# Hymba block on one core: scores of head group B over 128 rows with zeroed partner rows, one softmax factor on ScalarE, adaLN tiles packed closer

## The chip, the core and the metric

One core of a Trainium2 chip runs one launch of the kernel. The metric is the device time in microseconds, taken as the median over runs. Five engines matter here: the tensor engine (PE, with PEld for its weight loads), VectorE (DVE), ScalarE (ACT), GpSimd (POOL) and SyncE (SP, which issues most DMAs). Each works through its own queue in order, and semaphores join them.

## The reference

One decoder layer over 512 tokens, model width 2048, all in 32-bit floats. Eight heads of group A use dilated windows; eight heads of group B use differential attention, which is where the change lies:

```python
def differential_attention(q, k, v, lam):
    # q, k: (B, S, 2, H, e): two maps, e = 64; v: (B, S, H, 128)
    ...
        s = jnp.einsum('bqmhe,bkmhe->bmhqk', qblk, k)        # one block of 128 queries
        s = jnp.where(causal, s, -jnp.inf)
        a = jax.nn.softmax(s, axis=-1)
        attn = a[:, 0] - lam * a[:, 1]
        return jnp.einsum('bhqk,bkhe->bqhe', attn, vf)
...
mod = silu(c) @ w_ada + b_ada                                # adaLN: six vectors of 2048
h = rmsnorm(x, g_pre_attn) * (1.0 + sc_a) + sh_a
proj = h @ w_in                                              # q, k, v of both groups
...                                                          # rope, both attentions, per-head rmsnorm
x = x + gt_a * rmsnorm(mix @ w_out, g_post_attn)
h = rmsnorm(x, g_pre_ffn) * (1.0 + sc_f) + sh_f
x = x + gt_f * rmsnorm((silu(h @ w_gate) * (h @ w_up)) @ w_down, g_post_ffn)
```

A score of group B thus contracts over 64 numbers, and every head has two score maps.

## The kernel before

**Large products.** Weights and activations are split into a rounded part and a rest (`w_hi` on ScalarE at L1709, `w_lo` on VectorE at L1718), and each product is three fast ones (L277 to L279 with the activations stationary, L282 to L284 with the weights stationary). Attention itself works in plain 32-bit floats.

**Steps.** After a first phase the program is a list of steps. A projection step (0 to 79) takes one 128x1024 weight tile and issues 24 fast products of 512 columns; an output-projection step (80 to 143) issues 12; then comes the feed-forward part. The main loop at the end of `body` writes each step in this order: things that start a step (`start_ev`, among them the copies of finished projections to SBUF and the DMAs that swap rows for the rotary part), attention on the tensor engine (`pe_ev`), the first half of the step's products, the split on ScalarE for the tile two steps ahead (`do_hi`), transposes and copies (`mid_ev`, `mid_act`), the second half, then VectorE's work (`post_ev`, `post_late`, `do_lo`), then the small adaLN tiles (`aux`), then `post_end`. Nothing reorders afterwards, so an engine's queue stands in this order.

**Attention units.** `place_unit` puts a unit into a step. For group B a unit is one block of 128 queries of one head: head h, block b stands in step 20 + 4h + b, so the 32 units fill steps 20 to 51. `unit_stages` gives its parts. `s0` (same step, ahead of the step's products): the two score products (L507; head h uses rows 64(h mod 2) to 64(h mod 2)+63 of its pair's tile for both maps), mask and maximum on VectorE (L512), exponential with its sum on ScalarE (L516). `s0b` (late in the step) is

```python
dve.reciprocal(stt[:, 6:8], stt[:, 4:6])                                  # L521
dve.tensor_scalar(stt[:, 0:1], stt[:, 7:8], nlam, None, op0=OP.mult)      # L522: the factor of map 1
dve.tensor_scalar(p1(), p1(), stt[:, 0:1], None, op0=OP.mult)             # L523
dve.scalar_tensor_tensor(p0(), p0(), stt[:, 6:7], p1(), ...)              # L524
```

One step later come the transposes (L529) and their copy (L534), two steps later the value products (L545, first thing on the tensor engine). When a head's last block is done, `head_post` normalises it: copy (L558), largest value, squares on ScalarE (L568), four small operations (L581 to L584), and a step later the scaling (L589, L590), its transposes later still (L595). For head h the copy, the squares and the four small operations fall into the step of block 1 of head h+1, and on VectorE they stand ahead of that block's factor.

**Rotary.** `evac_rope_at` makes three long VectorE operations (L426 to L428) per half pair of heads. A planner puts them into steps 17, 18, 22, 23, 25, 26, 30, 34, 46 and 50 within group B's stretch, ahead of that step's factor.

**adaLN tiles.** 96 tiles of 512 KB (and 32 more much later) are multiplied and summed on VectorE (L228). They share a ring of four `raw` buffers with the weights, in the order of their use. The same planner adds them to steps while its running estimate of VectorE's time stays within `M_ADA` of the tensor engine's (`M_ADAW` from step 80 on); its estimates per unit are in `place_unit`. Steps 0 to 10 also hold late shift tiles with VectorE work of their own, steps 4 to 14 a correction (L728).

**Tables.** `tabB` (made in `late_tab` at step 14) has four planes of 512 columns: cosine, sine, causal mask, and one unused.

Of the kernel before, what the change touches and what calls it, by code (L numbers as in the profile page):

```python
# [8 lines left out]
AF = mybir.ActivationFunctionType  # L9
OP = mybir.AluOpType  # L10
# [11 lines left out]
LATE_KC = [KORDER[s] for s in LATE_S]  # L22
KORDER2 = [kc for kc in KORDER if kc not in LATE_KC] + LATE_KC
M_ROPE = 1.0
M_ADA = -0.05
M_ADAW = 0.8
M_AV = -1.0
M_DMA = 0.7
# [6 lines left out]
def body(tc, t):  # L35
    nc = tc.nc
    pe, act, dve, pool, sync = nc.tensor, nc.scalar, nc.vector, nc.gpsimd, nc.sync
# [3 lines left out]
    with ctx:  # L41
# [8 lines left out]
        def U(tag, shape, dt=F, name=None):  # L50
            return up.tile(shape, dt, tag=tag, name=name or tag)

        def PS(b, shape=(128, 512)):
            return pp.tile(list(shape), F, tag=f"b{b}", name=f"b{b}")
# [275 lines left out]
        QK = {}  # L330
# [62 lines left out]
        tabB = {}  # L393
# [78 lines left out]
        def pt_store(head, i):  # L472
            u, c = PT_AT[head, i]
            if u not in pts:
                pts[u] = U(PT_UNIT[u], [128, 2048], name=f"pts{u}")
            return pts[u][:, c:c + (384, 384, 512)[i]]

        def unit_stages(n, kind, head, qbs):
            W = sum(128 * (qb + 1) for qb in qbs)
            offs = [0, 128][:len(qbs)]  # L480
            d = {}
            p0 = lambda: misc["p"][:, n % 2, :W]
            p1 = lambda: misc["p"][:, 2 + n % 2, :W]
            last = kind == "A" and head >= 4

            def s0():
                stt = sp.tile([128, 8], F, name="stt", tag="stt", bufs=4)
                d["st"] = stt
                lst = []
                for j, qb in enumerate(qbs):  # L490
                    N = 128 * (qb + 1)
                    qs = slice(128 * qb, 128 * qb + 128)
                    ms_ = slice(128 * (3 - qb), 512)
                    r = slice(offs[j], offs[j] + N)
                    if kind == "A":
                        if j == 0:
                            sc = PS(4 + n % 2)
                        qk = QK[f"A{head // 2}"]
                        i = 2 * (head % 2)
                        pe.matmul(sc[:, r], qk[:, i, qs], qk[:, i + 1, :N], start=True, stop=True)  # L500
                        lst.append((sc[:, r], p0()[:, r], lc[:, ms_], SCALE_A, HEADST[kind, head]["den"][:, qb:qb + 1]))
                    else:
                        qk = QK[f"B{head // 2}"]
                        k = slice(64 * (head % 2), 64 * (head % 2) + 64)
                        for m in range(2):
                            sc = PS(4 + m)
                            pe.matmul(sc[:, :N], qk[k, 2 * m, qs], qk[k, 2 * m + 1, :N], start=True, stop=True)  # L507
                            lst.append((sc[:, :N], p0() if m == 0 else p1(), tabB["t"][:, 2, ms_], SCALE_B,
                                        stt[:, 4 + m:5 + m]))
                for m, (sc, p, mask, scale, den) in enumerate(lst):  # L510
                    mx = stt[:, m:m + 1]
                    dve.tensor_tensor_reduce(p, sc, mask, op0=OP.add, op1=OP.max, scale=1.0,  # L512
                                             scalar=-3e38, accum_out=mx)
                    nm = stt[:, 2 + m:3 + m]
                    dve.tensor_scalar(nm, mx, -scale, None, op0=OP.mult)
                    act.activation(p, p, AF.Exp, bias=nm, scale=scale, accum_out=den)  # L516

            def s0b():
                if kind == "B":
                    stt = d["st"]  # L520
                    dve.reciprocal(stt[:, 6:8], stt[:, 4:6])  # L521
                    dve.tensor_scalar(stt[:, 0:1], stt[:, 7:8], nlam, None, op0=OP.mult)  # L522
                    dve.tensor_scalar(p1(), p1(), stt[:, 0:1], None, op0=OP.mult)  # L523
                    dve.scalar_tensor_tensor(p0(), p0(), stt[:, 6:7], p1(), op0=OP.mult, op1=OP.add)  # L524

            def s1():
                tr = PS(6, (128, 4, 128))
                for j in range(W // 128):
                    pe.transpose(tr[:, j, :], misc["p"][:, n % 2, 128 * j:128 * j + 128], ident)  # L529
                d["tr"] = tr  # L530

            def s1b():
                d["pt"] = pt_store(head, max(qbs) - 1) if last else misc["pt"][:, n % 2, :W]
                act.activation(d["pt"], d["tr"][:, :W // 128, :], AF.Copy)  # L534

            def s2():
                h = HEADST[kind, head]
                if qbs[0] == 0:
                    h["pv"] = PS(head if last else 7, (128, 4, 128))
                v = V[f"V{kind}{head // 4}"]  # L540
                e = slice(128 * (head % 4), 128 * (head % 4) + 128)
                o = 0
                for qb in qbs:
                    for j in range(qb + 1):
                        pe.matmul(h["pv"][:, qb, :], d["pt"][:, o:o + 128], v[:, j, e], start=j == 0, stop=j == qb)  # L545
                        o += 128
            return s0, s0b, s1, s1b, s2

        HEADST = {}
# [52 lines left out]
        pe_cost = defaultdict(float)  # L602
        dve_cost = defaultdict(float)

        def place_unit(n, kind, head, qbs, hn, s):
            s0, s0b, s1, s1b, s2 = unit_stages(n, kind, head, qbs)
            m = 1 if kind == "A" else 2
            for qb in qbs:
                N = 128 * (qb + 1)
                pe_cost[s] += m * max(0.218, 0.00168 * N)  # L610
                dve_cost[s] += m * (0.4 + N / 960) + (1.0 + 1.6 * N / 960 if kind == "B" else 0)
                pe_cost[s + 1] += 0.107 * (qb + 1)
            if 0 in qbs:
                def mk(kind=kind, head=head):
                    h = HST[kind, head]
                    hs = sp.tile([128, 5, 4], F, name="hst", tag="hst", bufs=4)
                    for i, k in enumerate(("den", "ss", "f", "rd", "nb")):
                        h[k] = hs[:, i, :]
                pe_ev[s].append((0, mk))
            pe_ev[s].append((2, s0))  # L620
            post_late[s].append(s0b)
            mid_ev[s + 1].append(s1)
            mid_act[s + 1].append(s1b)
            if kind == "A" and head >= 4:
                late_pv[head].append(s2)
                assert s + 1 < W0
                return
            for qb in qbs:
                pe_cost[s + 2] += 0.218 * (qb + 1)
            pe_ev[s + 2].append((0, s2))  # L630
            if 3 in qbs:
                a, b, c, c2, d = head_post(kind, head, hn)
                start2_ev[s + 2].append(a)
                mid_act[s + 2].append(b)
                post_late[s + 2].append(c)
                post_ev[s + 3].append(c2)
                pe_ev[s + 4].append((1, d))
                dve_cost[s + 2] += 1.0 if kind == "A" else 1.6
                dve_cost[s + 3] += 0.8
                pe_cost[s + 4] += 0.43  # L640
# [18 lines left out]
        post_end = defaultdict(list)  # L659
# [102 lines left out]
        for part in range(2):  # L762
            start_ev[14 + part].append(lambda part=part: late_tab(part))
# [6 lines left out]
        def late_tab(part):  # L770
            if part == 0:
                tabB["t"] = U("R3", [128, 4, 512], name="tabB")
                sync.dma_start(tabB["t"][:, 2, :], t["cb"])
            for p in range(0, 128, 32):
                o = 64 * ((p // 32) % 2) if part else 0
                sync.dma_start(tabB["t"][p:p + 32, part, :], (sin_a if part else cos_a)[o:o + 64:2, :])
# [92 lines left out]
        for jj, kp in enumerate(KP_ORDER):  # L869
            for k in range(2):  # L870
                kc = 2 * kp + k
                s = wsteps[0, 0, jj, 0]
# [177 lines left out]
        for h in range(4, 8):  # L1050
            s = W0 + 1 + (h - 4)
# [4 lines left out]
        for i in range(W0 + 60):  # L1056
            mm_t = 5.13 if i < W0 else 2.57
            if todo:
                hn, k, h, qbs = todo[0]
# [20 lines left out]
            t_dma = max(t_dma, t_pe) + 1.45 * (1 + len(aux[i]))  # L1080
            while ada_todo and i < W0 + 46 and i >= 1 and t_dve + 1.14 <= t_end + (M_ADA if i < W0 else M_ADAW) and \
                    t_dma + 1.45 <= t_end + M_DMA and len(aux[i]) < NAUX:
# [554 lines left out]
        for c in range(2):  # L1637
            p = dpos
# [137 lines left out]
        for i in range(NSTEP):  # L1776
# [10 lines left out]
            s = steps[i]  # L1787
# [146 lines left out]
```

## Time and profile before

| What | Value |
|---|---|
| median of 3 runs | 2191.88 us (2189.95 to 2193.71) |
| profiled execution, its span | 2191.79 us, 2190.0 us |
| tensor engine busy | 2150.6 us |
| VectorE, ScalarE, GpSimd busy | 1672.8, 1058.8, 103.7 us |
| steps 20 to 51 (group B's units) | about 229 to 484 us |
| steps 80 to 143 (output projection) | about 677 to 870 us |

Times on the timeline count from the span's start. In a timeline row stand the start, the duration, engine and line, what is written and read, shapes, how many instructions were merged (the duration is then that of all), and in brackets the idle time before it with what ended it. A 32-bit product appears as two instructions. Matmuls overlap by more than a third of a recorded duration, so distances between starts say how long the engine was taken. Rows of groups give count, busy time and mean nanoseconds.

### The profile page before, as it was taken

The page shows a single profiled execution, that of the slowest core. Times are in us where ns is not written, and L with a number is a line of the kernel's source. Part 1 is how long each engine was busy: PE and PEld are TensorE (multiplying, and loading weights), DVE is VectorE, ACT ScalarE, POOL GpSimd, SP SyncE. Part 2 cuts the span into 40 slices and gives each one's busy share as a digit, 9 for nine tenths or more (in the row PEclk, how much of TensorE's full clock was granted, in tenths as well). Part 3 has the DMA queues.
Part 4 walks back from the last instruction along what each step waited for, and adds up shares of the span by engine and source line. Part 5 has one row for each costly group of instructions (what it writes and reads, how often), then busy time and mean ns, then how long its engine had stood idle before and what let it go on. Part 6 is the DMA issues. An engine that isn't in the chain of part 4 may idle for free.

```text
span 2190.0 us, 26905 instructions
## 1 busy us (share of the span) xinstructions
PE 2150.6 (98%) x9748; PEld 1756.7 (80%) x9748; DVE 1672.8 (76%) x2337; ACT 1058.8 (48%) x1541; POOL 103.7 (5%) x112
## 2 busy tenths in 40 slices
PE   7999999999999999999999999999999999999997
PEld 6888777778888888787888888888888888888886
DVE  6987777776767775796777677777777787798888
ACT  5444344444435565654555554555554544443443
POOL 0000000001001000000001011000100000000000
PEclk8999999999999999999999999999999999999999
DMA  9797634555678877888779769778877889999997
GB/s 374 297 347 228 167 113 155 167 155 175 215 232 272 291 248 255 265 284 231 221 219 281 227 203 278 221 209 253 250 220 213 278 332 396 337 386 362 345 338 268
DMA packets 160452, 564.39 MB, mean 258 GB/s; under 512 B 17440, under 2 KB 17728, under 8 KB 153920
## 3 DMA queue, kind: packets, MB, share of 16 engines
q1 hardware_dynamic: 142608, 502.09, 63.8%
q0 software_dynamic: 10944, 39.85, 10.3%
q10 hardware_dynamic: 6768, 20.73, 3.2%
q8 instruction: 77, 1.26, 0.2%
q14 instruction: 55, 0.45, 0.1%
HBM read 499.67 MB, written 54.02 MB: 253 GB/s over the span
## 4 chain that ended last, share of the span: by engine, by line
PE 87%; DMA 5%; DVE 5%; ACT 1%; issue 1%; ACTq 0%; POOL 0%; SPq 0%; DVEq 0%; POOLq 0%
PE b L283 22%; PE b L282 22%; PE b L284 22%; PE b L277 5%; PE b L279 5%; PE b L278 5%; PE b L507 2%; DMA w_raw<-in_wout 1%; DMA a<-acts 1%; DVE w_lo L1718 1%; PE b L545 1%; PE b L1276 1%; PE b L500 1%; PE b L529 1%; ACT w_hi L1709 1%
## 5 line engine op out<-in xcount | busy, mean ns | idle before, releaser
L1718 DVE TENSOR_TENSOR w_lo<-raw,w_hi 128x1024 fp32r<-128x1024 f32 x235 | 285.6, 1221 | 150.6 <-ACT w_hi L1709 150.3
L1709 ACT ACTIVATE w_hi<-raw 128x1024 fp32r<-128x1024 f32 x235 | 248.4, 1061 | 287.6 <-PE b L284 227.3
L282 PE MATMUL b<-w_hi,h 128*128 128x512 f32 x864 | 342.8, 397 | 0.4 <-ACT xT L212 0.4
L283 PE MATMUL b<-w_lo,h 128*128 128x512 f32 x864 | 337.0, 390 | 1.6 <-DVE w_lo L1718 1.5
L284 PE MATMUL b<-w_hi,h 128*128 128x512 f32 x864 | 336.9, 390 | 0.0
L1718 DVE TENSOR_TENSOR w_lo<-w_raw,w_hi 128x1024 fp32r<-128x1024 f32 x176 | 214.0, 1220 | 61.7 <-ACT w_hi L1709 61.6
L1709 ACT ACTIVATE w_hi<-w_raw 128x1024 fp32r<-128x1024 f32 x176 | 185.5, 1056 | 154.3 <-PE b L284 68.8
L282 PE MATMUL b<-w_hi,e 128*128 128x512 f32 x640 | 250.3, 391 | 3.9 <-ACT w_hi L1709 3.9
L283 PE MATMUL b<-w_lo,e 128*128 128x512 f32 x640 | 250.5, 391 | 0.6 <-DVE w_lo L1718 0.6
L284 PE MATMUL b<-w_hi,e 128*128 128x512 f32 x640 | 250.0, 391 | 0.0
L282 PE MATMUL b<-w_hi,a 128*128 128x512 f32 x616 | 240.1, 390 | 1.2 <-DMA a<-acts 1.2
L283 PE MATMUL b<-w_lo,a 128*128 128x512 f32 x616 | 240.0, 390 | 1.1 <-DVE w_lo L1718 1.1
L284 PE MATMUL b<-w_hi,a 128*128 128x512 f32 x616 | 239.8, 389 | 0.0
L277 PE MATMUL b<-h,w_hi 128*128 128x512 f32 x512 | 213.2, 416 | 0.0
L1709 ACT ACTIVATE w_hi<-w_lent 128x1024 fp32r<-128x1024 f32 x121 | 128.3, 1061 | 161.8 <-PE b L284 119.7
L278 PE MATMUL b<-h,w_hi 128*128 128x512 f32 x512 | 200.7, 392 | 2.9 <-DVE h L273 2.9
L279 PE MATMUL b<-h,w_lo 128*128 128x512 f32 x512 | 201.1, 393 | 0.0
L282 PEld LDWEIGHTS b<-w_hi,h 128*128 128x128 f32 x864 | 162.3, 188 | 37.1 <-issue 3.7
L283 PEld LDWEIGHTS b<-w_lo,h 128*128 128x128 f32 x864 | 162.4, 188 | 36.3 <-DVE w_lo L1718 3.4
L1718 DVE TENSOR_TENSOR w_lo<-w_lent,w_hi 128x1024 fp32r<-128x1024 f32 x121 | 147.5, 1220 | 55.3 <-ACT w_hi L1709 55.2
L284 PEld LDWEIGHTS b<-w_hi,h 128*128 128x128 f32 x864 | 162.2, 188 | 34.1
L282 PEld LDWEIGHTS b<-w_hi,e 128*128 128x128 f32 x640 | 120.8, 189 | 29.5 <-ACT w_hi L1709 4.4
(356 smaller groups left out, 3456.7 us busy)
## 6 DMA issues: line engine op xcount, KB each, us to landing
a<-acts SPq DMA_DIRECT2D x154, 512.0 KB, 5.2
raw<-in_wgu SPq DMA_DIRECT2D x131, 512.0 KB, 6.2
w_raw<-in_win SPq DMA_DIRECT2D x107, 512.0 KB, 5.0
w_raw<-in_adar SPq DMA_DIRECT2D x96, 512.0 KB, 4.6
w_lent<-in_wgu SPq DMA_DIRECT2D x69, 512.0 KB, 7.0
w_raw<-in_wout SPq DMA_DIRECT2D x64, 512.0 KB, 4.5
acts<-stage SPq DMA_DIRECT2D x49, 512.0 KB, 4.4
raw<-in_wds SPq DMA_DIRECT2D x47, 512.0 KB, 5.9
```

The costliest lines, as they stand in the source:

```text
L277: pe.matmul(ps, whi, ahi, start=start, stop=False, **kw)
L278: pe.matmul(ps, whi, alo, start=False, stop=False, **kw)
L279: pe.matmul(ps, wlo, ahi, start=False, stop=stop, **kw)
L282: pe.matmul(ps, ahi, whi, start=start, stop=False, **kw)
L283: pe.matmul(ps, ahi, wlo, start=False, stop=False, **kw)
L284: pe.matmul(ps, alo, whi, start=False, stop=stop, **kw)
L500: pe.matmul(sc[:, r], qk[:, i, qs], qk[:, i + 1, :N], start=True, stop=True)
L507: pe.matmul(sc[:, :N], qk[k, 2 * m, qs], qk[k, 2 * m + 1, :N], start=True, stop=True)
L529: pe.transpose(tr[:, j, :], misc["p"][:, n % 2, 128 * j:128 * j + 128], ident)
L545: pe.matmul(h["pv"][:, qb, :], d["pt"][:, o:o + 128], v[:, j, e], start=j == 0, stop=j == qb)
L1709: act.activation(hi, raw, AF.Copy)
L1718: dve.tensor_tensor(lo, raw, hi.bitcast(F), op=OP.subtract)
```

## The change

The fourth plane of `tabB` holds zeros in rows 64 to 127 of its first 256 columns (for even heads) and in rows 0 to 63 of the others (odd heads). At the end of the step before a unit, ScalarE copies the unit's query rows (64 rows, two maps of 128 columns) into the other half, and the score products contract over all 128 rows: the other head's keys meet zeros. The factor of map 1 is multiplied in by ScalarE. The planner's costs for group B's units are lowered and `M_ADA` goes from -0.05 to 0.5.

```diff
-M_ADA = -0.05
+M_ADA = 0.5
...
+        def qz_of(head):
+            return tabB["t"][:, 3, 256 * (head % 2):256 * (head % 2) + 256].rearrange("p (m q) -> p m q", m=2)
+
+        def qz_copy(head, qb):
+            k = slice(64 * (head % 2), 64 * (head % 2) + 64)
+            q = QK[f"B{head // 2}"].rearrange("p (m i) t -> p m i t", m=2)[k, :, 0, 128 * qb:128 * qb + 128]
+            act.activation(qz_of(head)[k], q, AF.Copy)
...
-                        k = slice(64 * (head % 2), 64 * (head % 2) + 64)
                         for m in range(2):
                             sc = PS(4 + m)
-                            pe.matmul(sc[:, :N], qk[k, 2 * m, qs], qk[k, 2 * m + 1, :N], start=True, stop=True)
+                            pe.matmul(sc[:, :N], qz_of(head)[:, m, :], qk[:, 2 * m + 1, :N], start=True, stop=True)
...
-                    dve.tensor_scalar(p1(), p1(), stt[:, 0:1], None, op0=OP.mult)
+                    act.activation(p1(), p1(), AF.Copy, scale=stt[:, 0:1])
...
-                pe_cost[s] += m * max(0.218, 0.00168 * N)
-                dve_cost[s] += m * (0.4 + N / 960) + (1.0 + 1.6 * N / 960 if kind == "B" else 0)
+                pe_cost[s] += m * max(0.222, (0.00168 if kind == "A" else 0.0009) * N)
+                dve_cost[s] += m * (0.4 + N / 960) + (0.8 + 0.8 * N / 960 if kind == "B" else 0)
...
+            if kind == "B":
+                post_end[s - 1].append(lambda: qz_copy(head, qbs[0]))
...
+                pool.memset(tabB["t"][64:128, 3, 0:256], 0.0)
+                pool.memset(tabB["t"][0:64, 3, 256:512], 0.0)
```

Twelve lines are added, so line numbers of the changed kernel are up to 12 higher. The units and the rotary steps stay in their steps. Of the 96 early adaLN tiles six move: steps 87, 88, 90, 91, 93 and 94 lose one each, steps 1, 2, 3, 13, 20 and 21 get one more.

ScalarE in step 25 (head 1, block 1), before: two exponentials, copy of head 0's result, split of a weight, squares, copy of transposes; then the next step's exponentials.

```order
L516 ACTIVATE misc_p,stt<-misc_p,stt 128x256 x2
L558 ACTIVATE misc_pt<-b_1900 128x512
L1709 ACTIVATE w_hi<-w_raw 128x1024
L568 ACTIVATE junk,hst<-misc_pt,hst 128x128 x4
L534 ACTIVATE misc_pt<-b_2105 128x128
L516 ACTIVATE misc_p,stt<-misc_p,stt 128x384 x2
```

The same place now:

```order
L524 ACTIVATE misc_p,stt<-misc_p,stt 128x256 x2
L566 ACTIVATE misc_pt<-b_1923 128x512
L1721 ACTIVATE w_hi<-w_raw 128x1024
L576 ACTIVATE junk,hst<-misc_pt,hst 128x128 x4
L542 ACTIVATE misc_pt<-b_2131 128x128
L531 ACTIVATE misc_p<-misc_p,stt 128x256
L485 ACTIVATE tabB<-B_950 64x256
L524 ACTIVATE misc_p,stt<-misc_p,stt 128x384 x2
```

The product by the factor (L531) and, behind it, the copy of the next unit's query rows (L485) stand between this step's work and the next step's exponentials.

VectorE in step 20 (head 0, block 0), from the reciprocal to the next unit's maximum, before:

```order
L521 RECIPROCAL stt<-stt 128x2
L522 TENSOR_SCALAR stt<-stt,lam_79 128x1
L523 TENSOR_SCALAR misc_p<-misc_p,stt 128x128
L524 SCALAR_TENSOR_TENSOR misc_p<-misc_p,stt 128x128
L1718 TENSOR_TENSOR w_lo<-w_raw,w_hi 128x1024
L228 SCALAR_TENSOR_TENSOR w_raw,red<-w_raw,silu_b 128x1024
L512 ISA misc_p,stt<-b_1850,tabB 128x256
```

and now:

```order
L529 RECIPROCAL stt<-stt 128x2
L530 TENSOR_SCALAR stt<-stt,lam_79 128x1
L532 SCALAR_TENSOR_TENSOR misc_p<-misc_p,stt 128x128
L1730 TENSOR_TENSOR w_lo<-w_raw,w_hi 128x1024
L228 SCALAR_TENSOR_TENSOR w_raw,red<-w_raw,silu_b 128x1024
L228 SCALAR_TENSOR_TENSOR w_raw,red<-w_raw,p_82 128x1024
L520 ISA misc_p,stt<-b_1869,tabB 128x256
```

L523 has left VectorE, so the operation behind it (now L532) waits for ScalarE, and a second adaLN tile (L228) has come in.

VectorE in the output projection, from the scaling of the last group A head on (steps 86 to 90), before:

```order
L590 TENSOR_TENSOR misc_p<-misc_p,hst 128x512
L228 SCALAR_TENSOR_TENSOR w_raw,red<-w_raw,silu_b 128x1024
L1718 TENSOR_TENSOR w_lo<-w_raw,w_hi 128x1024
L228 SCALAR_TENSOR_TENSOR w_raw,red<-w_raw,p_82 128x1024
L1718 TENSOR_TENSOR w_lo<-w_raw,w_hi 128x1024
L843 TENSOR_TENSOR mixlo_5203<-mixT_5538,mixhi_5202 128x256 x2
L228 SCALAR_TENSOR_TENSOR w_raw,red<-w_raw,silu_b 128x1024
L1718 TENSOR_TENSOR w_lo<-w_raw,w_hi 128x1024 x2
```

and now:

```order
L598 TENSOR_TENSOR misc_p<-misc_p,hst 128x512
L228 SCALAR_TENSOR_TENSOR w_raw,red<-w_raw,silu_b 128x1024
L1009 TENSOR_TENSOR red<-red 128x16
L1014 TENSOR_TENSOR gsh<-red,cst 128x16
L1730 TENSOR_TENSOR w_lo<-w_raw,w_hi 128x1024 x2
L855 TENSOR_TENSOR mixlo_5255<-mixT_5590,mixhi_5254 128x256 x2
L1730 TENSOR_TENSOR w_lo<-w_raw,w_hi 128x1024 x2
```

The tile of step 86 is now the last of the 96; from there on the splits of the weights follow each other without one in between.

## The prediction

> **What bounds the kernel now.** I read the page's busy times first, then the chain that ended last, then the engines' busy time over the stretch in which head group B is scored.
>
> ```profile
> PE 2150.6 (98%) x9748; PEld 1756.7 (80%) x9748; DVE 1672.8 (76%) x2337; ACT 1058.8 (48%) x1541; POOL 103.7 (5%) x112
> ...
> PE 87%; DMA 5%; DVE 5%; ACT 1%; issue 1%; ACTq 0%; POOL 0%; SPq 0%; DVEq 0%; POOLq 0%
> ...
> 229.00:484.00 255.00, 253.73 (x1162) 193.90 (x1160) 196.51 (x508) 112.47 (x279) 7.06 (x7) 1.00 0.50 149
> ```
>
> The tensor engine carries the end: 98% busy, 87% of the chain, and in the 255 us of head group B (third row; the columns after the length are PE, PEld, DVE, ACT, POOL, granted clock, DMA share, GB/s) it has 1.3 us idle at full clock. So two things count: tensor time that goes away, and new waits of the tensor engine. VectorE and ScalarE matter only through the second.
>
> **Tensor time that goes away.** The timeline of the tensor engine shows the stream around a 256-wide unit of group B (step 21, scores between the first two rows), a 512-wide one (L507, step 23) and one of group A (L500).
>
> ```profile
> 235.68 0.39 PE L279 MATMUL b<-h,w_lo 128*128 128x512 f32 x1
> ...
> 237.39 0.40 PE L278 MATMUL b<-h,w_hi 128*128 128x512 f32 x1
> ...
> 251.60 0.60 PE L545 MATMUL b<-VB,misc_pt 128*128 128x128 f32 x4
> 252.14 1.98 PE L507 MATMUL b<-B 64*128 64x512 f32 x4
> ...
> 254.38 0.39 PE L278 MATMUL b<-h,w_hi 128*128 128x512 f32 x1
> ...
> 498.38 1.02 PE L500 MATMUL b<-A 128*128 128x512 f32 x2
> ...
> 499.47 0.39 PE L278 MATMUL b<-h,w_hi 128*128 128x512 f32 x1
> 499.70 0.40 PE L279 MATMUL b<-h,w_lo 128*128 128x512 f32 x1
> ```
>
> Streamed products start 0.23 us apart (499.47 to 499.70), so the one ahead of 499.47 began in earnest at 499.24: one 128-row product of 512 columns took 0.86 us. A value product (L545) takes 0.11 (eight of them, below, span 0.45 more than these four). The B unit therefore had the engine from 251.60 + 4 x 0.11 = 252.04 to 254.38 - 0.23 = 254.15, or 2.11 us, where two products at group A's rate are 1.72. The 256-wide unit had it from 235.91 to 237.16, 1.25 us, where two are 0.86. The excess is 0.39 both times: a 64-row product is no slower per column, but the unit pays about 0.40 us at its two ends, when the array goes between 128 and 64 rows; the row at 252.14 starts 0.1 late, the rest I split so that half of the excess lies ahead of the scores. With zero rows every product has 128 rows and the unit looks like group A's. I take the 0.40 for all 32 units (8 heads x 4 query blocks): **-12.8 us**. The bound below is nothing saved, above 0.40 each.
>
> **The new waits.** The order shows what they hang on. ScalarE now does, in one queue: the product by the factor (it waits for the factor from VectorE's L522), then the copy of the next unit's query rows; and the next unit's scores wait for that copy. Before, they waited for no factor. So the question is when the factor is ready against when the tensor engine gets to the next scores. Head 4, block 1 (step 37):
>
> ```profile
> 362.68 1.05 PE L545 MATMUL b<-VB,misc_pt 128*128 128x128 f32 x8
> 363.66 1.13 PE L507 MATMUL b<-B 64*128 64x256 f32 x4
> 370.45 0.38 PE L545 MATMUL b<-VB,misc_pt 128*128 128x128 f32 x2
> 370.76 1.55 PE L507 MATMUL b<-B 64*128 64x384 f32 x4
> ...
> 364.40 0.42 DVE L512 CUSTOM_DVE_ANT_0 misc_p<-b,tabB 128x256 f32<-128x256 f32 x1 [1.51 <-PE b L507]
> 370.00 0.16 DVE L581 SCALAR_TENSOR_TENSOR hst<-hst 128x4 f32<-128x4 f32 x1 [2.20 <-ACT junk L568]
> 370.61 0.21 DVE L522 TENSOR_SCALAR stt<-stt,lam 128x1 f32<-128x1 f32 x1
> 371.25 0.48 DVE L524 SCALAR_TENSOR_TENSOR misc_p<-misc_p,stt 128x256 f32<-128x256 f32 x1
> ```
>
> The factor is ready at 370.82, after the next scores are due. It is not VectorE's load that makes it late: VectorE idled 1.51 us before L512 and 2.20 before L581. It is a chain: scores, maximum, exponentials, the finished head's squares on ScalarE (L568), its sums (L581 on), and only then the factor. The prices of what is put behind it are not in the trace; the nearest rows are:
>
> ```profile
> L516 ACT ACTIVATE misc_p<-misc_p,stt 128x256 f32<-128x256 f32 x24 | 12.2, 509 | 36.6 <-DVE stt L515 29.9 <-DMA swp<-B 6.6
> L516 ACT ACTIVATE misc_p<-misc_p,stt 128x384 f32<-128x384 f32 x24 | 14.8, 617 | 63.3 <-DVE stt L515 53.1 <-DVE hst L575 9.0 <-DMA w_raw<-in_adar 1.2
> L842 ACT ACTIVATE mixhi<-mixT 128x256 fp32r<-128x256 f32 x32 | 11.4, 403 | 0.0
> ...
> 366.09 0.58 ACT L558 ACTIVATE misc_pt<-b 128x512 f32<-128x512 f32 x1
> 366.57 1.05 ACT L1709 ACTIVATE w_hi<-w_raw 128x1024 fp32r<-128x1024 f32 x1
> ...
> 243.53 0.26 ACT L534 ACTIVATE misc_pt<-b 128x128 f32<-128x128 f32 x1
> 243.84 0.49 PE L545 MATMUL b<-VB,misc_pt 128*128 128x128 f32 x2 [0.91 <-ACT misc_pt L534]
> ```
>
> The product by a per-row factor is like the exponential with its per-row bias (0.51 us at 256 columns, 0.62 at 384), the copy of 256 columns like L842 (0.40). Neighbours on ScalarE overlap by 0.1 (366.09 + 0.58 against 366.57). A hand-over takes 0.05 (243.79 to 243.84), and a tensor wait also uncovers a weight load of 0.11 (the 0.49 of that pair against 0.38 at 370.45). From factor to next scores: 0.05 + 0.41 + 0.40 + 0.05 + 0.11 = 1.02 us, 1.13 at 384 columns. Bounds: 0.8 if both run like the cheapest copies (L534: 0.26), 1.25 if each hand-over is 0.15.
>
> *Block 1 of heads 2 to 7.* Count from when the engine is free for the scores: 362.68 + 8 x 0.11 = 363.56. The factor comes 7.26 later, 7.06 without the drain ahead of the scores, so the next scores can start at 8.08. The engine is free for them after 370.67 - 363.56 = 7.11, now 0.40 less, 6.71. It waits 1.37: six times, **+8.2 us**.
>
> *Block 2 of heads 2, 3, 6 and 7*, where VectorE also has a rotary step before the factor (head 3, step 34):
>
> ```profile
> 339.03 1.55 PE L507 MATMUL b<-B 64*128 64x384 f32 x4
> 347.33 1.98 PE L507 MATMUL b<-B 64*128 64x512 f32 x4
> ...
> 338.88 0.21 DVE L522 TENSOR_SCALAR stt<-stt,lam 128x1 f32<-128x1 f32 x1
> 339.52 0.48 DVE L524 SCALAR_TENSOR_TENSOR misc_p<-misc_p,stt 128x256 f32<-128x256 f32 x1
> 348.05 0.21 DVE L522 TENSOR_SCALAR stt<-stt,lam 128x1 f32<-128x1 f32 x1
> ...
> 251.39 0.22 DVE L522 TENSOR_SCALAR stt<-stt,lam 128x1 f32<-128x1 f32 x1
> 275.56 1.55 PE L507 MATMUL b<-B 64*128 64x384 f32 x4
> 276.75 0.21 DVE L522 TENSOR_SCALAR stt<-stt,lam 128x1 f32<-128x1 f32 x1
> ```
>
> From factor to factor 9.17 us of VectorE work, plus 0.18 because L524 now starts after ScalarE (0.61 instead of 0.43): 9.35, and 1.13 more to the scores, 10.48. The engine starts block 2 at 1.02 and needs 347.33 - 339.03 - 0.40 = 7.90: free at 8.92. It waits 1.56: four times, **+6.2 us**. The factors of blocks 0 and 3, and of block 2 in heads 4 and 5, come 2 to 5 us before they are needed: no wait.
>
> *Heads 0 and 1.* In head 1 block 1 has a rotary step (factor 276.96, next scores 275.56): it waits 2.7, and block 2 another 0.4. In head 0 the row at 243.84 is a wait for ScalarE's swap transfers that the earlier units' 0.8 us only lengthens, and the copy adds 0.3: 1.1. Then block 2 (factor 251.61, ahead of the scores at 252.14): VectorE comes to its factor about 1.9 later, for a second adaLN tile in step 21 (1.15) and a late, longer wait for ScalarE in block 1 (0.7), so the scores can start at 251.61 + 1.9 + 1.13 = 254.6, where the tensor engine is free at about 252.2: 2.4. Sum **+6.6 us**, the softest term: 3 to 9.
>
> **The six adaLN tiles** leave steps 87 to 94, where weights and tiles share four buffers, and go to steps 1, 2, 3, 13, 20 and 21; no unit and no rotary step changes its step.
>
> ```profile
> 721.20 0.50 PE L283 MATMUL b<-w_lo,mixhi 128*128 128x512 f32 x1 [0.49 <-DVE w_lo L1718]
> 730.01 0.50 PE L283 MATMUL b<-w_lo,mixhi 128*128 128x512 f32 x1 [0.36 <-DVE w_lo L1718]
> ...
> 197.80 0.16 DVE L685 TENSOR_TENSOR lam<-ld 128x1 f32<-128x1 f32 x1 [4.58 <-ACT ld L682]
> ```
>
> Both waits go: 0.85, and about 0.45 with the weight loads they uncover: **-1.3 us** (0.5 to 3). Where they arrive, steps 1 to 13 put at most 4 x 1.15 = 4.6 us on VectorE, which idles 4.58 us at 193 anyway; the split weights are made two steps (11 us) ahead until then. I count nothing; without that cover it would be up to 2 us. The two memsets lie on GpSimd, 5% busy: nothing. VectorE loses the 0.35 us L523, but waits longer than that for ScalarE, so no gain there.
>
> **Sum.** -12.8 + 8.2 + 6.2 + 6.6 - 1.3 = +6.9 us against the profiled execution's 2191.79 us (span 2190.0 and 1.8 around it; the median is 2191.88): **2198.7 us**. The bounds: hand-over price 12 x (-0.2 to +0.2), heads 0 and 1 -3.6 to +2.4, tiles -1.7 to +0.8: 2191 to 2204.
>
> A rule of the Trainium skill is about the step I charge most for. The page "ScalarE: Activation LUTs", section "Rules for kernel authors", says to multiply on VectorE, not on ScalarE. The trace agrees for this size (0.35 us at L523, 0.51 for L516). With the product left on VectorE the copy would not queue behind it, each wait would be 0.4 shorter, and the sum about 2194.
>
> **Rivals.** *The copy is never late.* If it ended before the tensor engine is free, the drains and tiles alone would count: 2191.8 - 14.1 = 2177.7 us, faster. It takes a factor ready 1.0 us before the next scores; blocks 0 and 3 have that, block 1 misses it by 1.4. 9%. *Gains and waits cancel.* Waits shorter by the lower price, heads 0 and 1 at 3: 2190 to 2195 us, 22%. *The long waits cool the clock.* A wait halved it once:
>
> ```profile
> 1010.77 0.79 PE L282 MATMUL b<-w_hi,e 128*128 128x512 f32 x1 [3.93 <-ACT w_hi L1709]
> ...
> 1011.00:1015.00 4.00, 3.53 (x8) 2.45 (x9) 4.00 (x4) 2.24 (x3) 0.00 (x0) 0.50 0.52 195
> ```
>
> After 3.93 us idle the granted clock was 0.50 for over 4 us, about 3 us lost. My waits of 2.4 and 2.7 in heads 0 and 1 lie below that; if both reach it, 2202 to 2205 us, 14%. The page "TensorE: Matmul & The Clock Gate", section "Why this matters for your kernels", asks for no idle gap over some 3 us; by it my two are just short. *The drains stay* although the rows are zero: 2198.7 + 12.8, less the 3 to 5 us by which a later engine waits less: 2207 us, 5%.
>
> **How the numbers follow.** The forecast, 2194 to 2203, has 50%. Within 0.2% (4.4 us, about what a measurement of this kernel can tell from no change) lie the cancelling case and the forecast's low end: 29%. Faster: the first rival, 9%. Slower: 62%. The range 2189 to 2206 leaves out the first and the last rival.
>
> **What would show it.** In the changed profile the scores of group B as 128x128 products with no gap at either end; waits of the tensor engine for ScalarE's copy, about 1.4 us each, in block 1 of nearly every head and in block 2 of four; none in blocks 0 and 3; steps 91 and 94 without waits. I am wrong if the copy's waits are missing or under 0.5 us, if the two early heads wait twice as long, or if steps 4 to 19 show tensor waits for split weights.

## The result, and the profile after

The changed kernel took 2208.99 us (median of 4 runs, 2207.93 to 2211.9) against 2191.49 us for the kernel before on the same chip: a ratio of 1.0083, interval 1.0071 to 1.0094. It is slower by 17.5 us. The forecast was slower by 6.9 us, 2198.7 us, and the measured time lies above the range. The profiled execution took 2207.93 us, its span is 2206.0 us. The busy times and the chain that ended last, from the page after:

```profile
PE 2147.0 (97%) x9748; PEld 1760.2 (80%) x9748; DVE 1659.8 (75%) x2305; ACT 1087.1 (49%) x1605; POOL 104.3 (5%) x114
...
PE 76%; DVE 13%; DMA 5%; ACT 4%; issue 1%; ACTq 0%; SPq 0%; POOL 0%; DVEq 0%; POOLq 0%
```

VectorE stands on the chain with 13% where it had 5%. The span grew by 16.0 us while all engines are about as busy as before, so the time went into waits.

**The drains went.** The tensor engine's timeline around the first unit of head 4, before:

```profile
355.20 0.83 PE L545 MATMUL b<-VB,misc_pt 128*128 128x128 f32 x6
355.95 0.71 PE L507 MATMUL b<-B 64*128 64x128 f32 x4
...
356.93 0.40 PE L283 MATMUL b<-w_lo,h 128*128 128x512 f32 x1
```

and after:

```profile
367.44 0.83 PE L553 MATMUL b<-VB,misc_pt 128*128 128x128 f32 x6
368.11 0.61 PE L515 MATMUL b<-B,tabB 128*128 128x128 f32 x4
...
368.79 0.40 PE L283 MATMUL b<-w_lo,h 128*128 128x512 f32 x1
```

From the first value product to the second streamed product it is 1.73 us before and 1.35 now. The same products, compared over all units, show 0.20 us less ahead of the scores and 0.19 less behind them, 0.39 a unit, 12.5 us in all.

**The waits came.** The tensor engine's waits from 195 to 500 us, before and after (columns: total, how often, the longest):

```profile
PE b L545 <- ACT misc_pt L534: 0.9, 1, 0.9
PE b L529 <- ACT tabs L1020: 0.4, 1, 0.4
```

```profile
PE b L515 <- ACT tabB L485: 17.0, 14, 2.5
PE b L553 <- ACT misc_pt L542: 3.4, 6, 0.8
PE b L746 <- DVE VB L678: 1.2, 1, 1.2
PE b L537 <- ACT tabs L1032: 1.1, 1, 1.1
```

The first row is the wait that was forecast, for the copy of the query rows. The other three were not. The timeline of head 4's blocks 0 and 1 after (step 36 and 37, the same place as in the prediction) shows how they arise:

```profile
370.61 0.21 DVE L530 TENSOR_SCALAR stt<-stt,lam 128x1 f32<-128x1 f32 x1
...
371.97 0.60 ACT L542 ACTIVATE misc_pt<-b 128x512 f32<-128x512 f32 x1 [0.64 <-PE b L537]
...
372.46 0.39 ACT L531 ACTIVATE misc_p<-misc_p,stt 128x128 f32<-128x128 f32 x1
...
372.89 0.35 DVE L532 SCALAR_TENSOR_TENSOR misc_p<-misc_p,stt 128x128 f32<-128x128 f32 x1 [2.06 <-ACT misc_p L531]
...
375.43 1.03 PE L515 MATMUL b<-B,tabB 128*128 128x256 f32 x4
...
376.58 0.42 DVE L520 CUSTOM_DVE_ANT_0 misc_p<-b,tabB 128x256 f32<-128x256 f32 x1
...
382.06 0.25 ACT L542 ACTIVATE misc_pt<-b 128x128 f32<-128x128 f32 x1
...
382.37 0.49 PE L553 MATMUL b<-VB,misc_pt 128*128 128x128 f32 x2 [0.27 <-ACT misc_pt L542]
...
382.80 0.22 DVE L530 TENSOR_SCALAR stt<-stt,lam 128x1 f32<-128x1 f32 x1
383.05 0.51 ACT L531 ACTIVATE misc_p<-misc_p,stt 128x256 f32<-128x256 f32 x1 [0.74 <-DVE stt L530]
383.46 0.40 ACT L485 ACTIVATE tabB<-B 64x256 f32<-64x256 f32 x1
...
383.92 1.56 PE L515 MATMUL b<-B,tabB 128*128 128x384 f32 x4 [1.06 <-ACT tabB L485]
```

In block 0 the factor (L530) is ready at 370.82, but ScalarE comes to the product (L531) only at 372.46: in its queue the copy of the transposes (L542) stands ahead, and that waits for the tensor engine. VectorE stands still for 2.06 us in front of the combine (L532). So in block 1 it reaches the maximum (L520) 1.15 us after the scores began, where before it was 0.74. The exponentials, the finished head's squares and with them L542 come later: value products wait as well, and so the next factor is ready 7.59 us after the scores began (375.43 to 383.02), not 7.16 as before. From there on it is close to the forecast: factor, product, copy, scores within 0.90 us (forecast 1.02).

Sorted into the terms of the prediction's sum (starts of the same tensor products in both traces, kept apart by unit; "late combine", "early factor" and "factor on VectorE" are experiments, below):

| us against the kernel before | forecast | after | late combine | early factor | factor on VectorE |
|---|---|---|---|---|---|
| drains, 32 units | -12.8 | -12.5 | -12.5 | -12.5 | -12.5 |
| block 1 of heads 2 to 7 | 8.2 | 13.0 | 8.6 | 4.0 | 3.0 |
| block 2 of heads 2, 3, 6, 7 | 6.2 | 6.3 | 3.6 | 0.0 | 0.0 |
| heads 0 and 1 | 6.6 | 6.9 | 3.9 | 0.8 | -0.6 |
| other units | 0 | 1.1 | 0.4 | 1.1 | 0.6 |
| steps 0 to 19 | 0 | 3.1 | 5.2 | 2.9 | 4.3 |
| behind group B, to 1000 us | -1.3 | -2.6 | -3.4 | -1.4 | -1.9 |
| ahead of step 0, and the rest | 0 | 0.7 | 1.0 | 0.0 | 1.8 |
| sum (profiled spans) | 6.9 | 16.0 | 6.9 | -5.1 | -5.3 |

### The profile page after: what moved, and what is told of

The parts are those of the page before. It is cut to its first block, busy times and chain, and to the rows that moved or that the text cites. A ratio compares the mean times of both kernels' runs of the same rounds, so it can differ in the third digit from the quotient of the medians.

```text
span 2206.0 us, 26961 instructions
## 1 busy us (share of the span) xinstructions
PE 2147.0 (97%) x9748; PEld 1760.2 (80%) x9748; DVE 1659.8 (75%) x2305; ACT 1087.1 (49%) x1605; POOL 104.3 (5%) x114
## 3 DMA queue, kind: packets, MB, share of 16 engines
q0 software_dynamic: 10944, 39.85, 10.1%
## 4 chain that ended last, share of the span: by engine, by line
PE 76%; DVE 13%; DMA 5%; ACT 4%; issue 1%; ACTq 0%; SPq 0%; POOL 0%; DVEq 0%; POOLq 0%
PE b L283 21%; PE b L284 21%; PE b L282 21%; PE b L277 3%; PE b L279 3%; PE b L278 3%; DVE w_lo L1730 3%; DVE w_raw L228 2%; DMA a<-acts 1%; DVE late_sh L228 1%; DMA w_raw<-in_adar 1%; PE b L1288 1%; ACT w_hi L1721 1%; PE b L509 1%; PE b L515 1%
## 5 line engine op out<-in xcount | busy, mean ns | idle before, releaser
L277 PE MATMUL b<-h,w_hi 128*128 128x512 f32 x512 | 218.2, 426 | 0.0
L278 PE MATMUL b<-h,w_hi 128*128 128x512 f32 x512 | 201.8, 394 | 2.4 <-DVE h L273 2.4
```

Source lines behind the costliest of these rows:

```text
L277: pe.matmul(ps, whi, ahi, start=start, stop=False, **kw)
L278: pe.matmul(ps, whi, alo, start=False, stop=False, **kw)
```

## The experiments

Each ratio below is against the kernel before on the same chip, where that took 2190.1 to 2191.5 us; not all experiments ran on one chip. Two theories stood after the comparison of the traces. Theory 1: the copy is late because it queues behind the product by the factor (the prediction's own reason). Theory 2: VectorE's wait for ScalarE's product is the delay, and the copy is only a place where it shows. A third, that the moved tiles make VectorE late, was tried beside them.

**The copy early.** The next unit's query rows are copied ahead of the weight split.

```diff
-                post_end[s - 1].append(lambda: qz_copy(head, qbs[0]))
+                early_act[s - 1].append(lambda: qz_copy(head, qbs[0]))   # runs ahead of do_hi
```

> The copy of the next unit's query rows moves ahead of the weight split on ScalarE, so it stands before the product by the factor and hangs on nothing that is late; all else is the changed kernel. Theory 1 (the copy is late because it queues behind the product by the factor): the waits of the scores for the copy, 17.0 us in 14 places, go; the 3.4 us of waits of the value products for the copy of the transposes stay: 2190 to 2196 us. Theory 2 (VectorE's wait of about 2 us per unit for ScalarE's product is the real delay, and the copy only the place where it shows): the waits move to the value products, and half of the gain at most comes back: 2199 to 2205 us. If neither counts (the copy itself is what costs): 2207 to 2210 us.

Measured: 2206.75 us, ratio 1.0079 (1.0064 to 1.0095): no gain to speak of. The tensor engine's waits from 195 to 505 us no longer name the scores; the first row is now

```profile
PE b L553 <- ACT misc_pt L542: 16.8, 16, 2.3
```

The waits only moved, from the scores to the value products. Theory 1 alone falls: the copy hangs on nothing late here, and the time is nearly the same. Theory 2 expected 2199 to 2205 us, and its upper end lies 1.75 us below what came; by the time alone, the copy itself could still be the cost.

**The product back on VectorE.**

```diff
-                    act.activation(p1(), p1(), AF.Copy, scale=stt[:, 0:1])
+                    dve.tensor_scalar(p1(), p1(), stt[:, 0:1], None, op0=OP.mult)
```

> The product by the factor goes back to VectorE; copy, zero rows and moved tiles as in the changed kernel. Theory 1 and 2 agree that the waits shrink, but not on how far. Theory 1 (queue behind the product): the copy then ends about 0.35 us after the copy of the transposes, some 0.1 to 0.4 us after the engine is free for the scores, so block 1 waits 0.1 to 0.4 us, block 2 not at all: 2186 to 2192 us. Theory 2 (VectorE's waits for ScalarE): the same gain in block 1, and the waits of the value products for the copy of the transposes go too; nearer 2186. If VectorE's load were the cause (the moved tiles), the product on VectorE would make it worse: over 2209 us.

Measured: 2184.8 us, ratio 0.9974 (0.9965 to 0.9984), 24 us less than the changed kernel by one line. Both theories had this gain, and the time lies 1.2 us below the lower end of either, so this run does not choose between them; that VectorE's load is the cause (over 2209 us) falls. No score waits for a copy any more; the tensor engine's waits from 195 to 500 us are

```profile
PE b L746 <- DVE VB L678: 2.5, 1, 2.5
PE b L553 <- ACT misc_pt L542: 1.6, 3, 1.0
PE b L537 <- ACT tabs L1032: 0.4, 1, 0.4
```

**The old tile plan** (M_ADA and the planner's costs of the kernel before; all else changed).

```diff
-M_ADA = 0.5
+M_ADA = -0.05
```

> The planner's costs and M_ADA of the kernel before, so that no adaLN tile moves; zero rows, copy and factor on ScalarE as in the changed kernel. Theory 1: the tiles cost 2.9 us at step 16, 1.1 us at step 44 (the transposes of an adaLN row that now come there) and about 1.5 us of the wait between steps 22 and 23, and gain 2.5 us in the output projection: 2205 to 2208 us. Theory 3 (the six tiles make VectorE late in all of group B, and so cause the block 1 waits): 2196 to 2201 us.

Measured: 2212.38 us, ratio 1.0106 (1.009 to 1.0122). Both expectations missed: without the moved tiles it is not faster, if anything 3 us slower. Its profiled execution, at 2216.78 us the slowest of four, shows no wait at step 16, but longer ones in group B: 4.2 us of a value product in step 21, and 2.9 and 1.1 us at block 1 of head 6. The granted clock (last section) was at half for 20.5 us between 246 and 461 us, against 6.8 us in the changed kernel. At half speed that is an estimated 6 us more, which is more than the 3 us; in all four runs the mean granted clock was 0.989, against 0.991 to 0.992 in the changed kernel. So the tiles don't cause the waits of block 1; why some waits are longer here stays open.

**Zero rows alone** (factor on VectorE and the old tile plan).

> Only the zero rows and their copy: the factor on VectorE, the old planner costs. The tensor engine saves 12.5 us in 32 units. Theory 1: block 1 waits 0.1 to 0.4 us for the copy in 6 heads and perhaps 2 us in heads 0 and 1: 2180 to 2184 us. Theory 2: the same, 2179 to 2183 us. If the copy in ScalarE's queue costs by itself what it cost in the changed kernel: 2190 to 2200 us.

Measured: 2185.73 us, ratio 0.998 (0.997 to 0.9989), 4.4 us less than before. The median lies 1.7 us above the expected range. The profiled execution is the fastest of the ten; its span, 2180.6 us, is 9.4 us shorter than that of before, 12.5 us of drains less 2.4 of new waits in block 1 and smaller ones. The first part of the change is a gain, even with its copy on ScalarE.

**The factor on ScalarE alone**, in the kernel before.

```diff
-                    dve.tensor_scalar(p1(), p1(), stt[:, 0:1], None, op0=OP.mult)
+                    act.activation(p1(), p1(), AF.Copy, scale=stt[:, 0:1])
```

> The kernel before with one edit: the product by the factor on ScalarE. 64-row scores, no copy, no moved tile. Theory 1 (the copy queued behind the product is what is late): there is no copy, so no change, 2188 to 2194 us. Theory 2 (VectorE waits about 2 us in each unit for ScalarE's product, so the next maximum, and with it everything behind it, comes late): waits of the value products for the copy of the transposes as in the run with the early copy, some 17 us: 2203 to 2212 us.

Measured: 2196.61 us, ratio 1.0022 (1.0013 to 1.0032). Slower, as theory 2 says, but by 5.3 us where 12 to 21 were expected: both theories missed the size. Alone, the two parts of the change are worth -4.4 and +5.3 us, which makes +0.9; together they cost 17.5 with the moved tiles and 22.3 without them (the old tile plan, against 2190.1 us). VectorE's waits from 215 to 500 us bear on why. Before, for ScalarE's exponentials and for the tensor engine's scores:

```profile
DVE stt L521 <- ACT misc_p L516: 20.0, 16, 4.2
...
DVE misc_p L512 <- PE b L507: 8.2, 12, 1.9
```

The same list with the factor on ScalarE alone (L524 is the combine), and then with the changed kernel:

```profile
DVE misc_p L524 <- ACT misc_p L523: 34.1, 32, 1.7
DVE stt L521 <- ACT misc_p L516: 16.7, 16, 3.0
```

```profile
DVE misc_p L532 <- ACT misc_p L531: 39.1, 32, 2.3
DVE stt L529 <- ACT misc_p L524: 18.0, 16, 2.4
...
DVE misc_p L520 <- PE b L515: 1.2, 2, 0.6
```

Before, VectorE waits 8.2 us for scores: there the tensor engine sets the pace, and a delay on VectorE is covered. With the product on ScalarE it waits 34.1 us for it in 32 units, 1.07 us each, the row for the scores is gone, and the tensor engine waits 3.0 us for value products in five places. The reading is that VectorE and ScalarE, waiting for each other, set the pace around these places, where the kernel is already slower than the tensor engine at its old speed, and that a faster tensor engine gains nothing there. The row for the scores alone does not show it: it is 1.6 us also with the factor on VectorE, in a kernel faster than the one before.

**The combine late.** Product and copy stay on ScalarE as in the changed kernel; VectorE does the combine behind the step's weight split and tiles, so it no longer stands in front of it.

```diff
-                    dve.scalar_tensor_tensor(p0(), p0(), stt[:, 6:7], p1(), ...)   # in s0b
...
+            post_end[s].append(s0c)                                    # s0c: that operation
```

> The changed kernel, but VectorE does the operation that waits for ScalarE's product (L532) only behind the step's weight split and adaLN tiles, so that it no longer waits there; the product stays on ScalarE, the copy stays behind it. Theory 1: the scores still wait for the copy, no change: 2206 to 2211 us. Theory 2: VectorE's 2 us waits go, the maxima come in time, block 1 waits 1.2 to 1.5 us instead of 2.3 and the value products no longer wait: 2199 to 2205 us.

Measured: 2199.42 us, ratio 1.0038 (1.0028 to 1.0047): 9.6 us of the loss are back, as theory 2 says. Two rows of VectorE's waits in the same stretch (the combine is L535 in this kernel):

```profile
DVE misc_p L520 <- PE b L515: 17.6, 19, 1.8
...
DVE misc_p L535 <- ACT misc_p L531: 0.3, 1, 0.3
```

VectorE's wait for the product is gone, and no value product waits. Its wait for the scores is partly theirs for the copy, which costs the tensor engine 13.4 us here. Block 1 of heads 2 to 7 now waits 1.03 to 1.74 us, 8.6 in all, which is what the prediction charged for it.

**Combine late and copy early.**

> Both edits: the late combine and the early copy. The early copy alone gave 2206.75 us. Theory 2: with VectorE no longer waiting, the early copy frees the scores too, and nothing waits but a few value products: 2182 to 2190 us, although the product is still on ScalarE. If the product on ScalarE costs by ScalarE's own time and not by the wait: 2197 to 2207 us.

Measured: 2186.0 us, ratio 0.9973 (0.9961 to 0.9985). The early copy, worth 2 us (within the uncertainty) with VectorE waiting, is worth 13 without. Theory 2, with theory 1 as its second half: only when VectorE does not wait is the copy's place what costs.

**The factor early.** Factor and product are written right behind the weight split, ahead of squares and transposes' copy; the combine stays, the copy still follows at the end of the step.

```diff
-            post_late[s].append(s0b)
+            early_act[s].append(s0b)        # behind do_hi, ahead of mid_act
+            post_late[s].append(s0c)
```

> The changed kernel with its engines as they are, the product by the factor on ScalarE too, but factor and product are written ahead of the finished head's squares and the transposes' copy, right behind the weight split; VectorE's combine (L532) stays in its place. The copy then queues behind the transposes' copy alone and VectorE finds the product done or nearly done. If place and not engine is what costs: VectorE's 39.1 us of waits for the product fall to 10 to 25 us, the scores wait for the copy less than 3 us in all: 2186 to 2196 us. If ScalarE's own time is what costs: 2200 to 2210 us.

Measured: 2187.59 us, ratio 0.9987 (0.9978 to 0.9996). VectorE's wait for the product, its row in the same list, has more than halved:

```profile
DVE misc_p L535 <- ACT misc_p L531: 16.7, 18, 1.5
```

Every engine does what it does in the changed kernel. Two places differ: the product's in ScalarE's queue, and the factor's in VectorE's, now ahead of the finished head's sums. Together they were worth 21 us; the run does not part them.

**The factor early, the combine late.** Here s0c goes into `post_end` instead.

> The same with the combine behind the step's split and tiles, so that VectorE doesn't wait at all. Theory 2: 2183 to 2188 us, no worse than with the product on VectorE (2184.8 us), perhaps 1 us better. If the product ahead of the transposes' copy makes the value products wait (0.4 us more in seven steps): 2187 to 2190 us.

Measured: 2186.63 us, ratio 0.9981 (0.9973 to 0.999), as good as with the product on VectorE, not better.

**A copy that nobody reads.** The run with the factor on ScalarE alone, and the early copy added; the scores contract over 64 rows and don't use it.

> What the copy costs while VectorE waits for ScalarE: the run with the factor on ScalarE alone (2196.61 us; 64-row scores, no moved tile) with the early copy added in ScalarE's queue, 32 times 0.41 us, of which 0.31 is not overlapped; its result is read by nobody, since the scores stay over 64 rows. If VectorE's loop through ScalarE sets the pace of this stretch, each copy lengthens it by up to 0.31 us: up to 9.9 us, 2202 to 2207 us. If the copy finds room (ScalarE is 48% busy): 2195 to 2199 us, and what the changed kernel loses beyond the factor's price comes from the tensor engine running ahead of VectorE once the drains are gone.

Measured: 2205.17 us, ratio 1.0062 (1.005 to 1.0075): 8.6 us for 32 copies of 0.41 us, although ScalarE is about half idle there (138 of 265 us busy). In the two traces group B is 6.7 us longer with the copy, and of that an estimated 1.7 us is one more stretch of 3.41 us at half clock (last section). So a copy costs 0.16 to 0.27 of its 0.31 us. This kernel still has its drains; the early copy run, which has none (and the moved tiles), takes 2206.75: without the drains nothing was gained there, as far as the moved tiles can be left out. So while VectorE and ScalarE set the pace, a faster tensor engine is worth little or nothing, and an operation put into ScalarE's queue is paid for half or more.

**Two tries for a better tile plan**, both with the factor on VectorE. First up to three tiles a step in steps 54 to 79, then a third tile in five steps from 70 to 78 only.

```diff
-                    t_dma + 1.45 <= t_end + M_DMA and len(aux[i]) < NAUX:
+                    t_dma + 1.45 <= t_end + M_DMA and len(aux[i]) < (3 if 54 <= i < W0 else NAUX):
```

> A better version, if the causes are right: zero rows and copy, factor on VectorE, old planner costs, and up to three adaLN tiles a step in steps 54 to 79 (two elsewhere), so that the last of the 96 is in step 78: none in the output projection and none in steps 1 to 13. Against zero rows only (2185.73 us) the waits of the output projection go, 1.3 to 3 us: 2181 to 2185 us. Rival: the third tile fills VectorE or the four buffers in steps 54 to 78, and weights come late there: 2186 to 2195 us.

> A better version, second try: zero rows and copy, factor on VectorE, the changed planner costs, but no tile ahead of step 17 beyond those of the kernel before, and a third tile only in steps 70, 72, 74, 76 and 78, so that the last of the 96 is in step 84. Against the factor on VectorE with the changed tiles (2184.8 us): the wait of 2.5 us at step 16 goes, the output projection stays without its waits for split weights: 2181 to 2184 us. Rival: steps 70 to 78 have no room for a third tile, as the version with 3 tiles from step 54 on showed (2199.85 us): 2185 to 2190 us.

Measured: 2199.85 us, ratio 1.0035 (1.0024 to 1.0045), and 2189.98 us, ratio 0.9996 (0.9987 to 1.0005). The rival came true for the first, 4.9 us beyond the upper end of its range, and the second came out at its upper end. In the list of the tensor engine's waits, the first has a new row of a weight product, where the output projection begins,

```profile
PE b L282 <- ACT VA L438: 6.1, 1, 6.1
```

and this stretch, from group B to 1000 us, lost 10.1 us; in the second it lost 1.1, where the factor on VectorE with the changed plan gained 1.9. The best versions tried are the factor on VectorE with the changed plan and the late combine with the early copy, 0.9974 and 0.9973 of the time before; the runs do not tell them apart, nor clearly from zero rows alone and the early factor with the late combine (0.998 and 0.9981).

## Why the prediction was wrong

**The tensor time (-12.8) was right**: 0.39 us a unit. That it could simply be added into the sum was not: it counts only where the tensor engine sets the pace.

**Block 1 of heads 2 to 7 (8.2 us) was mis-sized: 13.0.** The step that failed is the last of the tile part: "VectorE loses the 0.35 us L523, but waits longer than that for ScalarE, so no gain there". The wait was seen and charged nothing. It is 39.1 us in 32 units. The 4.8 us by which this term was short are half of the 9.1 us by which the profiled spans miss the sum; steps 0 to 19 are another 3.1. I took the factor's delay from the trace of before (7.26 us from scores to factor, 7.06 without the drain), in which VectorE reached the maximum in time, and even quoted the 1.51 us that it idles there; after the change VectorE's wait of 2.06 us in the unit before uses that cover up. The maximum comes 0.41 us later behind its scores, the factor 7.59 us behind them instead of 7.06, and value products wait besides. The late combine takes this wait away (0.3 us is left) by moving one operation: block 1 costs 8.6, as forecast. That its whole sum is 6.9 us, as forecast too, is luck: block 2 and heads 0 and 1 cost 5.3 us less than the forecast, steps 0 to 19 5.2 us more.

**Block 2 (6.2 us) was right: 6.3**, 1.56 to 1.58 us in each of the four places against 1.56. There the forecast had carried VectorE's time through the whole step. The late combine shortens it to 0.9 each.

**Heads 0 and 1 (6.6 us) came to 6.9, partly by luck.** Between steps 25 and 26 it is 2.8 (forecast 2.7), between 26 and 27 0.4 (0.4). Between 21 and 22, where 1.1 was charged, 0.6 were gained: the wait for L534 that stands there before did not come. Between 22 and 23 it is 4.1, not 2.4. The idle time itself was near the forecast, 2.2 to 2.4; the rest is clock (last section).

**The tiles (-1.3 us) had the wrong sign: +1.6.** In the output projection both waits for split weights are gone, and from group B to 1000 us the kernel gains 2.6 (forecast 1.3). But "VectorE idles 4.58 us at 193 anyway" was no cover. After the change the same row has this, with the ScalarE row that decides it and the tensor engine at step 16:

```profile
198.49 1.06 ACT L1721 ACTIVATE w_hi<-w_raw 128x1024 fp32r<-128x1024 f32 x1 [3.35 <-DMA w_raw<-in_win]
...
201.09 0.16 DVE L695 TENSOR_TENSOR lam<-ld 128x1 f32<-128x1 f32 x1 [3.90 <-ACT ld L692]
...
211.47 1.05 PE L746 MATMUL b<-junk,p 128*128 128x1 f32 x8 [1.19 <-DVE VB L678]
```

VectorE idles 3.90 us, and it comes out of it 3.29 us later than before (197.80). What it waits for stands on ScalarE behind a weight split, and that waits for its weight: weights and tiles share four buffers, which VectorE now hands back later (the weight split at 190.80 us before stands at 193.53). So the idle time moved with the work ahead of it. VectorE stays late until step 16, where the tensor engine waits for a copy to SBUF (L678). Every kernel with the changed tile plan lost 2.9 to 5.2 us by step 20, except the early copy with 0.9; those whose tiles up to there are the old ones lost none. Up to step 18 the kernels with the changed plan run the same program, so the size of this loss varies from execution to execution. In step 44 another 1.1 us come from the transposes of an adaLN row (L537 after L1032), which the earlier tiles brought there.

**The rivals.** That the copy is never late, or that gains and waits cancel, did not happen. Nor did the drains stay, though the time given for that, 2207, is near: it is the wrong cause. The cooled clock came in part. Of the signs of being wrong that the prediction named none came (the copy's waits are there, heads 0 and 1 cost 6.9 us, no tensor wait for a split weight in steps 4 to 19): none of them looked at VectorE's waits. The rule of the Trainium skill that I weighed ("ScalarE: Activation LUTs", section "Rules for kernel authors": multiply on VectorE) was worth 24 us here, not the 5 that I worked out from it. But the early factor, with the product still on ScalarE, is 2.8 us from it: what costs is its place, that VectorE waits for it and that the copy queues behind it.

## What to carry to other kernels

When an operation moves from one engine to another and the first must wait for its result, charge the wait to everything that stands behind it in the waiting engine's queue, into the next round of the loop, and check what covers it after the change, not before. Two changes that were worth -4.4 and +5.3 us alone cost 17 together. The runs fit this reason: one made the tensor engine faster, and the other took the setting of the pace from it. An idle time that ends on another engine's event is no room for more work if that work delays the event; and before moving an operation off the waiting engine, write the operation that needs its result later in the queue: one line brought back 9.6 us.

## What the runs showed of the hardware

The granted clock halved after shorter waits than I had taken for dangerous. In the forecast a wait of 3.93 us did it, and I thought waits of 2.4 and 2.7 safe. Two waits of the tensor engine after the change:

```profile
256.35 2.79 PE L515 MATMUL b<-B,tabB 128*128 128x512 f32 x4 [2.18 <-ACT tabB L485]
...
283.02 1.56 PE L515 MATMUL b<-B,tabB 128*128 128x384 f32 x4 [2.46 <-ACT tabB L485]
```

A third, at step 16, is of 1.19 us, with only one-column products behind it (the row at 211.47 above). The engines' busy times around the three, in pieces of 3.41 us (the first number after the length is the tensor engine, the third column from the right the granted clock):

```profile
209.60:213.01 3.41, 2.22 (x13) 1.45 (x12) 3.41 (x8) 1.31 (x2) 0.00 (x0) 1.00 1.01 302
213.01:216.42 3.41, 3.41 (x10) 2.66 (x9) 3.04 (x2) 1.08 (x2) 0.00 (x0) 0.50 0.79 269
...
253.98:257.39 3.41, 1.23 (x5) 0.57 (x4) 2.63 (x5) 0.92 (x2) 0.00 (x0) 1.00 0.05 19
257.39:260.80 3.41, 3.41 (x8) 2.00 (x7) 2.74 (x8) 1.52 (x4) 0.00 (x0) 0.50 0.48 154
...
277.87:281.28 3.41, 2.70 (x13) 1.99 (x11) 3.38 (x5) 2.06 (x9) 0.00 (x0) 1.00 0.08 32
281.28:284.69 3.41, 1.67 (x6) 1.09 (x7) 2.74 (x10) 0.92 (x2) 1.01 (x1) 1.00 0.00 0
284.69:288.10 3.41, 3.41 (x17) 2.77 (x16) 3.33 (x8) 2.71 (x6) 0.00 (x0) 1.00 0.47 154
```

After the waits of 1.19 and 2.18 us the clock was 0.50, after the longest one 1.00. At step 16 the products fell back by about 0.2 us each, eight times: some 1.6 us of the 3.1 at steps 0 to 19 are clock, and about as much of the 4.1 between steps 22 and 23. The Trainium skill, page "TensorE: Matmul & The Clock Gate", section "Why this matters for your kernels", warns of idle gaps over some 3 us; here gaps of 1.2 and 2.2 us were enough and one of 2.5 was not, so the length alone does not decide.

The record of the clock in the fourteen traces says more. Between 60 and 2150 us every stretch at half clock lasts 3.41 us or twice that, and within one trace these stretches begin whole multiples of 3.41 us apart; the pieces above are cut there. What can be compared is the idle time within the piece just ahead. The wait of 2.18 us lies in one piece. That of 2.46 us falls into two, which are idle for 0.71 and 1.74 us. Of all pieces at full clock, the 23 that were idle for 1.96 us or more were each followed by half the clock, and none idle for less than 1.04 us was. In between, ten were and others, up to 1.94 us idle, were not, so idle time is not all that counts. This is read from the traces; no run was made to move a wait across such a boundary.
